# New durations in the planner that orders a two-layer encoder's small work between its large products

## The chip, the core and the metric

The kernel runs on one core of one Trainium2 chip. The metric is the device time of one execution in microseconds (us). It is the median of several runs. Five engines work side by side, each with its own instructions in program order: TensorE (PE) multiplies, VectorE (DVE), ScalarE (ACT) and GpSimd (POOL) do elementwise work, and SyncE (SP) issues the loads.

## What is computed

Two layers over 256 tokens of width 2048, in fp32. Each layer has a norm, one wide input projection, three mixers whose outputs are concatenated, an output projection, and a feed-forward block.

```python
def hybrid_layer(x, ...):
    h = rms_norm(x, norm_mix)
    z = jnp.einsum('bsd,de->bse', h, w_in)
    (ml_q, ml_k, ml_v, ml_o, ml_g, mla_cq, mla_ckv, dil_q, dil_k, dil_v) = jnp.split(...)
    y_a = mlstm_mixer(...)      # 4 heads
    y_b = mla_mixer(...)        # 6 heads
    y_c = dilated_mixer(...)    # 6 heads
    y = jnp.concatenate([y_a, y_b, y_c], axis=-1)
    x = x + jnp.einsum('bse,ed->bsd', y, w_out)
    h = rms_norm(x, norm_ff)
    u = jax.nn.relu(jnp.einsum('bsd,df->bsf', h, w_ff1))
    return x + jnp.einsum('bsf,fd->bsd', u * u, w_ff2)
```

## The kernel before

Every large product is made of three products of fp32r operands: each weight tile of 128x1024 is loaded (`wst`), ACT copies its high part (`whi`, L239), DVE subtracts to get the low part (`wlo`, L241), and PE multiplies high by high, high by low and low by high. `Weights.next()` (L248) splits three tiles ahead. PE's large products write the tile `g`: nine input groups a layer (`in_group`, L405; eight weight tiles each, 12 products of 512 columns a tile), then the output projection (`out_proj`, L1065) and four chunks of the feed-forward (`ffn`, L1089).

The mixers' small work runs between the products of the input groups. Each piece (`mla_head` L623, `dil_prep` L704, `dil_head` L732, `ml_head` L915 and others) is a Python generator, and each `yield` ends a step. The order of all instructions is fixed when the program is built, by the planner `Stream` (L117). It holds a clock `clk`, which each PE product moves on by its assumed cost (L193, L198), and for each of ACT, DVE and POOL the time at which it is thought to be free. `Engine.__getattr__` (L86) looks up an operation's cost as (fixed, per element) in `COST` (L76) and calls `issue` (L129): the operation starts at the latest of the engine's free time, the clock, and the ends of what the same task issued on other engines, each with `MARGIN` = 0.4 us (L70) added. So within one step an operation on DVE or POOL is thought to start after ACT's part of the step, whether it needs it or not. A task is due again at the latest of these ends (L157). `pump` (L165), called after every three products of a token group (L400), issues the next step of each task that is due.

```python
last = self.cur.last
t = max([self.free[name], self.clk] + [v for k, v in last.items() if k != name])
self.free[name] = t + cost
last[name] = t + cost + MARGIN
```

Where a result is needed at once, `until` (L173) issues the steps of all tasks in the order in which they are due, with no product between, and sets the clock to each due time. That happens at the six hooks at which an MLA head starts (`MLA_AT`, L69: after tiles 3 and 7 of groups 2, 3 and 4, so 48 products apart; L1011, L1028). A head takes 3 of the `HALF` = 7 buffers of the pool `half` from `mla_head`'s start to its end, so at most two heads are under way: the hook of head 2 waits until head 0 is over, and so on. The hooks are called first to sixth below. One MLA head's PE steps are, in order, `mla_z` (24 products), `nkT`, `qrT`, `mla_s`, `pT`, `oT`. Its step at L649 to L657 has six squares on ACT and four copies on DVE; its step at L668 to L674 has four copies on ACT (`nk`) and the three POOL operations of `apply_rope` (L528). PE's steps of a dilated pair start with `dqkT`, after `apply_rope` on POOL at L726. PSUM has four banks for the mixers' PE results; `give(m=1)` returns one in the plan as soon as its last reading is issued.

Of the kernel before, what the change touches and what calls it, by code (L numbers as in the profile page):

```python
# [11 lines left out]
F32R = mybir.dt.float32r  # L12
# [60 lines left out]
class Engine:  # L73


    COST = {  # L76
        "activation": (0.16, 0.00083), "copy": (0.07, 0.00083), "tensor_tensor": (0.07, 0.00104),
        "scalar_tensor_tensor": (0.13, 0.00104), "tensor_scalar": (0.07, 0.00080), "tensor_copy": (0.07, 0.00104),
        "tensor_reduce": (0.07, 0.00104), "tensor_tensor_reduce": (0.07, 0.00104), "reciprocal": (0.07, 0.0066),
        "tensor_tensor_scan": (0.07, 0.00104), "memset": (0.07, 0.0004),  # L80
    }

    def __init__(self, stream, name, engine):
        self.s, self.name, self.e = stream, name, engine

    def __getattr__(self, f):  # L86
        fn = getattr(self.e, f)
        if f not in self.COST:
            return fn

        def call(*args, **kw):
            out = kw["in_"] if f == "tensor_reduce" else kw["out"] if "out" in kw else args[0]
            n = math.prod(out.shape[1:])
            fixed, each = self.COST[f]
            if self.name == "pool":
                fixed, each = 0.15, 2 * each
            self.s.issue(self.name, fixed + each * n)
            return fn(*args, **kw)  # L98

        return call  # L100
# [16 lines left out]
class Stream:  # L117
# [8 lines left out]
        self.tasks = []  # L126
        self.room = room

    def issue(self, name, cost):  # L129
        last = self.cur.last  # L130
        t = max([self.free[name], self.clk] + [v for k, v in last.items() if k != name])
        self.free[name] = t + cost
        last[name] = t + cost + MARGIN

    def product(self, cost):
# [54 lines left out]

def mm(c, out, lhsT, rhs, start, stop):
    n = out.shape[-1]
    c.s.product(n / 2400.0 * (1 if lhsT.dtype == F32R else 4) + 0.0025)  # L193
    c.nc.tensor.matmul(out, lhsT, rhs, start=start, stop=stop)  # L194


# [128 lines left out]
def mm3(c, out, l, r, start, stop):  # L325

    mm(c, out, l[0], r[0], start, False)
    mm(c, out, l[0], r[1], False, False)
    mm(c, out, l[1], r[0], False, stop)
# [1006 lines left out]
```

## Time and profile before

| | us |
|---|---|
| median of 3 runs | 2157.25 |
| lowest, highest | 2154.41, 2159.11 |
| the profiled execution's time | 2155.49 |
| its span (first to last instruction) | 2153.3 |
| PE busy | 2119.8 |
| DVE busy | 1322.4 |
| ACT busy | 1082.3 |
| POOL busy | 110.4 |

The profile is of one execution. "Busy" of PE overlaps in the pipeline, so the pitch from one product's start to the next's is what counts. "Idle before" is the time an engine stood still ahead of an instruction, with what released it. The span's stages are: start to 36, the first layer's input groups and mixers to about 290, its output projection to 380, its feed-forward to about 1093; the second layer follows in the same way, with its input groups to about 1358 and the end at 2153.

### The profile page before, as it was taken

The page shows a single profiled execution, that of the slowest core. Times are in us where ns is not written, and L with a number is a line of the kernel's source. Part 1 is how long each engine was busy: PE and PEld are TensorE (multiplying, and loading weights), DVE is VectorE, ACT ScalarE, POOL GpSimd, SP SyncE. Part 2 cuts the span into 40 slices and gives each one's busy share as a digit, 9 for nine tenths or more (in the row PEclk, how much of TensorE's full clock was granted, in tenths as well). Part 3 has the DMA queues.
Part 4 walks back from the last instruction along what each step waited for, and adds up shares of the span by engine and source line. Part 5 has one row for each costly group of instructions (what it writes and reads, how often), then busy time and mean ns, then how long its engine had stood idle before and what let it go on. Part 6 is the DMA issues. An engine that isn't in the chain of part 4 may idle for free.

```text
span 2153.3 us, 28894 instructions
## 1 busy us (share of the span) xinstructions
PE 2119.8 (98%) x10848; PEld 1804.9 (84%) x10848; DVE 1322.4 (61%) x1963; ACT 1082.3 (50%) x1883; POOL 110.4 (5%) x142
## 2 busy tenths in 40 slices
PE   8999999999999999999999999999999999999999
PEld 6788888888888888888887888888888888888887
DVE  7668755655564565565557687556546655655654
ACT  5666655543453444454456676554434434534442
POOL 6112100000000000000001121000000000000000
PEclk9999999999999999999999999999999999999999
DMA  7544455566656666566554444556565666566565
GB/s 228 189 141 126 154 175 181 187 194 190 193 186 195 194 188 193 190 192 196 178 174 142 143 128 153 174 189 192 186 198 189 190 191 195 187 195 194 187 200 162
DMA packets 109004, 389.89 MB, mean 181 GB/s; under 512 B 12352, under 2 KB 12480, under 8 KB 108608
## 3 DMA queue, kind: packets, MB, share of 16 engines
q1 hardware_dynamic: 107136, 384.97, 56.6%
q10 hardware_dynamic: 1728, 3.07, 0.4%
q8 instruction: 85, 1.39, 0.3%
q14 instruction: 55, 0.45, 0.1%
HBM read 385.90 MB, written 2.10 MB: 180 GB/s over the span
## 4 chain that ended last, share of the span: by engine, by line
PE 89%; ACT 4%; DVE 3%; POOL 2%; issue 1%; DMA 1%; POOLq 0%; ACTq 0%; DVEq 0%; SPq 0%
PE g L194 84%; ACT junk L98 1%; PE mla_z L194 1%; ACT whi L98 1%; DVE wlo L98 1%; POOL acc L98 1%; PE oT L194 1%; POOL sq L98 1%; DMA wst<-w_in 1%; PE xT L200 0%; PE pT L200 0%; PE dil_s L194 0%; PE mla_s L194 0%; POOL rp L98 0%; ACT dil_z L98 0%
## 5 line engine op out<-in xcount | busy, mean ns | idle before, releaser
L98 DVE TENSOR_TENSOR wlo<-wst,whi 128x1024 fp32r<-128x1024 f32 (+2 forms) x732 | 889.5, 1224 | 317.4 <-ACT whi L98 307.7
L98 ACT CAST whi<-wst 128x1024 fp32r<-128x1024 f32 (+2 forms) x732 | 761.2, 1043 | 539.7 <-PE g L194 402.5
L194 PE MATMUL g<-whi,u 128*128 128x512 f32 x2048 | 633.4, 389 | 0.0
L194 PE MATMUL g<-xg,whi 128*128 128x512 f32 x2048 | 489.8, 391 | 0.0
L194 PEld LDWEIGHTS g<-whi,u 128*128 128x128 f32 x2048 | 384.5, 188 | 79.6
L194 PEld LDWEIGHTS g<-xg,whi 128*128 128x128 f32 x2048 | 376.4, 188 | 72.8
L194 PE MATMUL g<-wlo,u 128*128 128x512 f32 x1024 | 398.4, 389 | 0.0
L194 PE MATMUL g<-whi,xg 128*128 128x512 f32 (+1 forms) x1152 | 371.7, 389 | 6.3 <-ACT whi L98 6.3
L194 PEld LDWEIGHTS g<-xg,wlo 128*128 128x128 f32 x2048 | 263.1, 191 | 12.1 <-ACT xg L98 2.0
L194 PE MATMUL g<-xg,wlo 128*128 128x256 f32 x2048 | 267.4, 283 | 1.1 <-ACT xg L98 1.1
L194 PEld LDWEIGHTS g<-whi,xg 128*128 128x128 f32 x1152 | 215.5, 189 | 44.0 <-ACT whi L98 6.3
L194 PEld LDWEIGHTS g<-wlo,u 128*128 128x128 f32 x1024 | 192.3, 188 | 39.8
L194 PE MATMUL g<-wlo,xg 128*128 128x512 f32 (+1 forms) x576 | 222.0, 385 | 3.3 <-DVE wlo L98 3.3
L98 ACT COPY ev<-g 128x256 f32<-128x256 f32 x128 | 48.0, 375 | 340.7 <-PE g L194 340.7
L98 DVE TENSOR_TENSOR ev<-g,ev 128x256 f32<-128x256 f32 x128 | 54.4, 425 | 229.8 <-ACT ev L98 229.7
L194 PE MATMUL g<-whi,y 128*128 128x512 f32 x512 | 162.8, 393 | 0.0
L194 PEld LDWEIGHTS g<-wlo,xg 128*128 128x128 f32 x576 | 109.1, 189 | 23.3 <-DVE wlo L98 6.7
L194 PEld LDWEIGHTS g<-whi,y 128*128 128x128 f32 x512 | 96.1, 188 | 19.7
L194 PE MATMUL g<-wlo,y 128*128 128x512 f32 x256 | 99.7, 389 | 0.0
L98 DVE SCALAR_TENSOR_TENSOR x<-g,r,x 128x512 f32<-128x512 f32 x64 | 45.8, 751 | 83.2 <-PE g L194 83.2
L98 DVE SCALAR_TENSOR_TENSOR ev<-ev 128x256 f32<-128x256 f32 x128 | 54.4, 425 | 4.4
L194 PEld LDWEIGHTS g<-wlo,y 128*128 128x128 f32 x256 | 48.1, 188 | 9.5
(206 smaller groups left out, 1199.1 us busy)
## 6 DMA issues: line engine op xcount, KB each, us to landing
wst<-w_ff SPq DMA_DIRECT2D x512, 512.0 KB, 4.2
wst<-w_in SPq DMA_DIRECT2D x128, 512.0 KB, 3.7
wst<-w_out SPq DMA_DIRECT2D x64, 512.0 KB, 4.2
wst<-w_in SPq DMA_DIRECT2D x16, 336.0 KB, 3.0
wst<-w_mla SPq DMA_DIRECT2D x12, 416.0 KB, 3.1
xt<-xT SPq DMA_DIRECT2D x8, 256.0 KB, 5.1
x<-x SPq DMA_DIRECT2D x2, 1024.0 KB, 7.1
out<-x ACTq DMA_DIRECT2D x8, 256.0 KB, 2.2
```

Source lines behind the costliest of these rows:

```text
L98: return fn(*args, **kw)
L194: c.nc.tensor.matmul(out, lhsT, rhs, start=start, stop=stop)
```

## The change

The table `COST` and what uses it get other numbers. Costs on ACT and DVE gain about 0.03 to 0.17 us of fixed time (reciprocal, scan and squares differ more), and each operation's engine is thought free 0.08 us before its end (`OVERLAP`). An ACT operation that also sums (`accum_out`) costs 0.2 us more (`READ`). POOL's operations cost 0.3 us and four times the element rate, instead of 0.15 and twice. A product of fp32r costs n/2400 + 0.0133 us instead of n/2400 + 0.0025, and one of plain fp32 n/1200 + 0.0025 instead of n/600 + 0.0025. No instruction is added or removed; `MARGIN`, the hooks and the pools stay.

```diff
     COST = {
-        "activation": (0.16, 0.00083), "copy": (0.07, 0.00083), "tensor_tensor": (0.07, 0.00104),
-        "scalar_tensor_tensor": (0.13, 0.00104), "tensor_scalar": (0.07, 0.00080), "tensor_copy": (0.07, 0.00104),
-        "tensor_reduce": (0.07, 0.00104), "tensor_tensor_reduce": (0.07, 0.00104), "reciprocal": (0.07, 0.0066),
-        "tensor_tensor_scan": (0.07, 0.00104), "memset": (0.07, 0.0004),
+        "activation": (0.26, 0.00086), "copy": (0.19, 0.00084), "tensor_tensor": (0.155, 0.00105),
+        "scalar_tensor_tensor": (0.20, 0.00107), "tensor_scalar": (0.16, 0.00080), "tensor_copy": (0.155, 0.00104),
+        "tensor_reduce": (0.155, 0.00104), "tensor_tensor_reduce": (0.24, 0.00105), "reciprocal": (0.15, 0.0062),
+        "tensor_tensor_scan": (0.155, 0.00205), "memset": (0.07, 0.0004),
     }
+
+    OVERLAP, READ = 0.08, 0.2
...
             if self.name == "pool":
-                fixed, each = 0.15, 2 * each
-            self.s.issue(self.name, fixed + each * n)
+                fixed, each = 0.3, 4 * each
+            elif self.name == "act" and kw.get("accum_out") is not None:
+                fixed += self.READ
+            self.s.issue(self.name, fixed + each * n, self.OVERLAP)
...
-    def issue(self, name, cost):
+    def issue(self, name, cost, overlap):
         last = self.cur.last
         t = max([self.free[name], self.clk] + [v for k, v in last.items() if k != name])
-        self.free[name] = t + cost
+        self.free[name] = t + cost - overlap
         last[name] = t + cost + MARGIN
...
-    c.s.product(n / 2400.0 * (1 if lhsT.dtype == F32R else 4) + 0.0025)
+    c.s.product(n / 2400.0 + 0.0133 if lhsT.dtype == F32R else n / 1200.0 + 0.0025)
```

## Rows read from the trace of the kernel before

**Rows 1.** Page, part 1: busy us (share of the span), instructions of each engine

```profile
PE 2119.8 (98%) x10848; PEld 1804.9 (84%) x10848; DVE 1322.4 (61%) x1963; ACT 1082.3 (50%) x1883; POOL 110.4 (5%) x142
```

**Rows 2.** Windows: length, then busy PE, PEld, DVE, ACT, POOL, PE clock, DMA

```profile
36.50:290.00 253.50, 243.23 (x1328) 207.04 (x1328) 185.00 (x418) 167.61 (x460) 39.38 (x53) 0.99 0.48 153
...
1125.00:1358.00 233.00, 224.38 (x1213) 189.70 (x1212) 173.63 (x395) 154.08 (x425) 34.62 (x39) 0.99 0.45 142
1448.00:2149.00 701.00, 701.00 (x3562) 599.89 (x3561) 403.80 (x481) 308.45 (x381) 0.00 (x0) 1.00 0.60 190
```

**Rows 3.** PE's waits over the whole span: us in total, times, longest

```profile
PE pT L200 <- DVE sm_e L98: 5.4, 2, 2.9
PE dqkT L200 <- POOL dil_z L98: 4.4, 4, 1.2
PE g L194 <- DVE wlo L98: 3.3, 7, 0.8
PE ml_w L194 <- DVE qrT_sb L98: 2.0, 2, 1.0
```

**Rows 4.** PE timeline, third hook: start, us, operation, count, [idle before, releaser]

```profile
98.72 0.65 PE L200 MATMUL nkT<-const,nk 128*128 128x128 f32 x4 [0.25 <-ACT nk L98]
101.83 1.17 PE L200 MATMUL pT<-const,sm_e 128*128 128x128 f32 x4 [2.46 <-DVE sm_e L98]
...
103.67 0.58 PE L194 MATMUL oT<-p_hi,mla_vh 128*128 128x256 f32 x1 [0.25 <-ACT p_hi L98]
...
105.63 0.36 PE L194 MATMUL mla_z<-whi,lat_hl 128*128 128x192 f32 x1
```

**Rows 5.** Windows: the stretch after that wait, columns as in rows 2

```profile
101.20:108.00 6.80, 5.78 (x24) 4.92 (x25) 3.98 (x9) 3.06 (x6) 0.00 (x0) 0.50 0.08 29
```

**Rows 6.** PE timeline: the first of three large products, and what follows them

```profile
119.53 0.39 PE L194 MATMUL g<-whi,xg 128*128 128x512 f32 x1
...
120.21 0.60 PE L200 MATMUL pT<-const,sm_e 128*128 128x128 f32 x4
```

**Rows 7.** POOL timeline: the rope of the second dilated pair, first layer

```profile
238.22 3.25 POOL L98 TENSOR_TENSOR rp<-dil_z,drope 128x256 f32<-128x256 f32 x2 [28.24 <-DVE dil_z L98]
241.54 1.58 POOL L98 TENSOR_TENSOR dil_z<-rp,rp 128x256 f32<-128x256 f32 x1
```

**Rows 8.** PE timeline: that pair's first transposes

```profile
243.18 1.09 PE L200 MATMUL dqkT<-const,dil_z 128*128 128x128 f32 x8 [1.23 <-POOL dil_z L98]
```

**Rows 9.** Groups by line and form: busy us, mean ns, idle before

```profile
L98 POOL TENSOR_TENSOR rp<-dil_z,drope 128x256 f32<-128x256 f32 x12 | 17.9, 1511 | 108.2 <-DVE dil_z L98 102.2 <-DVE ml_den L98 6.0
L98 POOL TENSOR_TENSOR rp<-qr,rope 128x128 f32<-128x128 f32 x24 | 17.7, 758 | 191.7 <-DVE qr L98 155.1 <-DVE sm L98 36.6
...
L98 ACT ACTIVATE nk<-mla_z,rs_y 128x128 f32<-128x128 f32 x48 | 13.6, 370 | 1.1 <-DVE qr L98 1.0
```

**Rows 10.** ACT timeline: head 0's first square, and what follows its sixth

```profile
70.73 0.27 ACT L98 ACTIVATE junk<-mla_z 128x128 f32<-128x128 f32 x1
...
72.88 1.05 ACT L98 CAST whi<-wst 128x1024 fp32r<-128x1024 f32 x1
```

**Rows 11.** ACT timeline: head 2's last two copies before `nkT`

```profile
117.79 0.62 ACT L98 ACTIVATE nk<-mla_z,rs_y 128x128 f32<-128x128 f32 x2
```

**Rows 12.** PE timeline: head 2's `nkT`, and head 3's `pT` and `oT` at the sixth hook

```profile
122.91 0.60 PE L200 MATMUL nkT<-const,nk 128*128 128x128 f32 x4
...
155.21 0.60 PE L200 MATMUL pT<-const,sm_e 128*128 128x128 f32 x4
...
157.03 0.60 PE L200 MATMUL nkT<-const,nk 128*128 128x128 f32 x4
157.38 0.36 PE L194 MATMUL oT<-p_hi,mla_vh 128*128 128x256 f32 x1
158.18 0.25 PE L194 MATMUL mla_z<-whi,lat_hl 128*128 128x192 f32 x1
```

**Rows 13.** DVE timeline: head 3's softmax scaling, the input of that `pT`

```profile
153.60 0.84 DVE L98 TENSOR_SCALAR sm_e<-sm_e,sm 128x256 f32<-128x256 f32 x2
```

## Prediction

> **What bounds the kernel now.** I read the page's busy times first, then the windows by stage, then PE's list of waits, and last the timelines around the longest waits. PE is the bound: it is busy for 98% of the span, the next engine, DVE, for 61% [rows 1]. In the second feed-forward PE is busy in all of its 701 us [rows 2], so nothing that only reorders other engines can gain there. The two stretches of input groups and mixers are the only place with something to win: PE stands still for 253.50 - 243.23 = 10.3 us in the first layer and 233.00 - 224.38 = 8.6 us in the second [rows 2].
>
> The waits there have three kinds, and the change meets them differently [rows 3]. The first is a PE step that the plan put ahead of its data: `dqkT` after POOL, 4.4 us in four waits. The second is a hook that forces a head to its end, so that PE has no product to put between the head's steps: `pT` after `sm_e`, 5.4 us in two waits, both at the third hook. There the steps `nkT`, `pT`, `oT` and the new head's `mla_z` follow each other without a large product [rows 4]. Behind that wait TensorE ran at its lower level, 1.2 GHz, a granted clock of 0.50 through 6.80 us [rows 5]. At half clock PE's 5.78 busy us did what some 2.9 us would do at 2.4 GHz, so about 2.9 us a layer are lost to the clock as well. The third kind is a hand-over of a PSUM bank (`ml_w` after `qrT_sb`, 2.0 us in two) or a late weight tile (`wlo`, 3.3 us in seven). The planner's bookkeeping has no entry for the first of these: a bank is free in the plan when its reading is issued, before and after.
>
> **The change, part by part.** Product cost: three products of 512 columns take 120.21 - 119.53 = 0.68 us [rows 6], so 0.227 each. The plan counted 512/2400 + 0.0025 = 0.2158, and will count 0.2266. Its clock was 5% slow; a step due L us ahead stood 1.05 L later in real time, and will stand L later. Taken alone this makes each step earlier by 5%.
>
> The rope of a dilated pair: the plan gave three POOL operations on 256 elements 3 x (0.15 + 2 x 0.00104 x 256) = 3 x 0.682 = 2.05 us, and `dqkT` was due 0.4 later, at 2.45 us (2.57 us of real products). The trace has 238.22 to 243.12, that is 4.9 us [rows 7]. PE reached `dqkT` early and waited 1.23 us [rows 8]. The new plan gives 2 x (1.375 - 0.08) + 1.375 + 0.4 = 4.37 us, so `dqkT` moves back by 1.8 us, six or nine products since tasks are looked at every three. That is more than the longest wait of 1.2 us. Products of the same group fill it, and later ones of the dilated chain have a whole group and the first half of the output projection before them: y[12] and up are first read in its ninth weight tile, 8 x 12 x 0.227 = 21.8 us after the last group. So the 4.4 us should go; I keep 2.2 to 4.4 as bounds, since a weight split queued before the rope on DVE may shift it by one tile.
>
> An MLA head: for the step with six squares the plan gave 4 x 0.266 + 2 x 0.213 = 1.49 us on ACT, then margin, four DVE copies of 0.203, and margin: 3.10 us. The new table gives 2.91 + 0.4 + 0.91 + 0.4 = 4.62, 1.5 us more. The trace has 72.88 - 70.73 = 2.15 us for the squares with their read-outs [rows 10], between 1.49 and 2.91. For the step with `nk` and the rope, the plan starts POOL only after ACT's four copies and the margin: 1.06 + 0.4 + 3 x 0.416 + 0.4 = 3.1 us before, 1.24 + 0.4 + (2 x 0.758 + 0.838) + 0.4 = 4.4 after, 1.3 us more. The ten other waits of a head (two means, two rsqrt parts, split of q and k, split of qr, maximum, exponentials, scaling, split of p) gain 0.1 to 0.5 each, 1.7 together. The chain from `mla_z` to `oT` grows from 17.4 us in the plan (18.3 real) to 21.9: each head's PE steps stand up to 3.6 us later.
>
> They weren't early. Head 2's `nk` ended at 117.79 + 0.62 = 118.41 [rows 11] and its `nkT` ran at 122.91 [rows 12], 4.5 us later; head 3's `sm_e` was ready at 154.44 [rows 13] and its `pT` ran at 155.21. So here the longer durations repair no wait. They push the heads towards the hooks that force them.
>
> What that costs differs by hook. At the third, the head is already forced from its maximum on, and the wait is the chain's own length; I put 0.3 us more on it. At the fourth, the steps left after the third hook's forcing grow by only some 0.2 us net of the clock: 0. At the fifth, `pT` is already forced; 0.5 us. At the sixth, six large products lie between `pT` and `nkT`/`oT` [rows 12] and cover the split of p; pushed back by over 1.4 us, `pT` comes behind them, and PE waits their 6 x 0.227 = 1.4 us. Together 2.2 us a layer, 4.4 in all. No row shows a head pushed so; the bounds are 0 (the due times fall into the same three products, or are forced at the same place) and the price of the third hook's wait, 2.46 us [rows 4], at each of the fourth to sixth hooks in both layers, 6 x 2.46 = 14.8. I take the value by the products that stand between, since rows 12 show them.
>
> Bank hand-overs and weight splits: which task takes a freed bank, and which DVE step stands before a `wlo`, changes by chance. The loads on SP stay at the same products, but their staging buffers come free after `wlo`, and so behind whatever the plan puts before it. 0, with bounds from -2.0 (both `ml_w` waits gone) to +3.3 (the weight waits double) [rows 3].
>
> The feed-forward, the output projection, the dilated heads' scores with their bias and the smaller recurrent steps get new dues as well: nothing, since PE has products without gap there [rows 2] and each result is read 20 us or more later; if that cover went, a feed-forward tile would cost the added 0.4 us once a chunk, eight in all, 3.2 us.
>
> A rule that speaks against one price for POOL: `rp` on 256 elements took 1511 ns in the mean and on 128 elements 758 [rows 9], against 1.375 and 0.838 in the new table. The Trainium skill, page GPSIMD Engine Reference, section Specifications, says that POOL shares its SBUF interfaces with VectorE and contends with VectorE instructions that read two SBUF inputs. By it the rope's length depends on which subtraction runs beside it. The sum by it would keep some of the `dqkT` waits, at most 2.2 us; the sum above goes by the rows.
>
> **The sum.** 2155.5 (the profiled execution's own time; 2.2 us of it lie around the span of 2153.3) - 4.4 + 4.4 + 0 = 2155.5. The median of the runs before stands 1.8 us above that execution, which would make 2157.3. I take the middle, 2156.5.
>
> **The rivals.** Faster: the dues move within the same three products at the hooks, the heads are forced where they were, and only the premature steps are mended: -4.4 for `dqkT` and -2.0 for `ml_w`, 2149 to 2151. For it: POOL's old price is the only one that was off by more than half [rows 7]. It goes to about 2145 if the third hook's wait also gets shorter, so that the clock stays at 2.4 GHz behind it and the 2 x 2.9 us come back [rows 5]; against that, the heads only get later.
>
> Slower: the hooks. If heads 1, 2 and 3 reach hooks four to six with their exponentials still to do, PE waits there as at the third, 2.46 us each, 14.8 in all: 2155.5 - 4.4 + 14.8 = 2166. It decides where a head's `pT` isn't issued before the last six products in front of its hook. For it: 3.6 us of delay a head against 1.4 us of products in between [rows 12]. Against it: at each hook all due steps are issued and the clock jumps, which takes back what the younger head has lost. The Trainium skill, page TensorE: Matmul & The Clock Gate, section HAM oscillation, says that a gap in PE's work puts the array back to half clock, which has to be paid at each such gap. The trace agrees at the third hook [rows 4, 5]; by it each new long wait would add up to 2.9 us, 2172 if one more a layer did.
>
> No effect: the order hardly changes, since steps are placed in units of three products (0.68 us) and the differences per step are 0.1 to 0.5 us; then 2157. Against it, the rope and the squares, 1.3 to 1.9 us.
>
> **How the numbers follow.** A measurement of this kernel can tell 0.2%, 4.3 us, from no change. Forecast of gain and loss in balance 0.33 and no effect 0.08: 0.41 within 0.2%. Faster 0.31: the rival with `dqkT` mended and the hooks held. Slower 0.28: the hooks. The range goes from the clock's case, 2145, to somewhat above the hooks without a second loss of clock, 2168; the likeliest case's own range is 2151 to 2161.
>
> **What would show it.** `dqkT` after `dil_z` gone from PE's waits, or below 2 us, shows the rope's step right. Waits of `pT` grown above 5.4 us, or new ones of `mla_s`, show the hooks' price; fewer large products between `pT` and `oT` before the sixth hook's `mla_z` shows its place. A granted clock below 1.00 in more or fewer than two stretches shows the clock's part. PE busy for less than the whole of the last 701 us would prove the claim on the feed-forward wrong. A total under 2149 with the `pT` wait gone would mean that later estimates shorten a forced chain, which I hold unlikely.

## The result and the profile after

The changed kernel takes 2178.7 us (median of 4, 2177.1 to 2183.4) against 2156.5 us, a ratio of 1.0106 with a 95% interval of 1.0086 to 1.0125. It is slower by 22 us, outside the range that was given. Its profiled execution has a span of 2174.8 us, 21.5 more than before. Medians here leave out the few executions that took over 2300 us.

The windows of the changed kernel come first: the two stretches of input groups and mixers and the last feed-forward. Columns are as in [rows 2]: length, busy us of PE, PEld, DVE, ACT and POOL, granted clock, DMA. The first two reach somewhat further than those of [rows 2], so the second block has the kernel before over the same stretches.

```profile
36.63:310.00 273.37, 255.91 (x1375) 218.47 (x1375) 189.24 (x423) 173.44 (x467) 36.60 (x53) 0.97 0.46 147
1105.00:1385.00 280.00, 264.87 (x1412) 225.68 (x1411) 190.73 (x427) 175.65 (x468) 31.95 (x39) 0.97 0.44 140
1470.00:2171.00 701.00, 700.75 (x3561) 599.46 (x3559) 403.66 (x481) 308.19 (x380) 0.00 (x0) 1.00 0.60 190
```

```profile
36.50:300.00 263.50, 253.23 (x1377) 215.54 (x1377) 190.65 (x425) 172.83 (x467) 39.38 (x53) 0.99 0.49 155
1105.00:1364.00 259.00, 250.38 (x1368) 214.07 (x1367) 187.76 (x422) 170.85 (x465) 34.62 (x39) 0.99 0.46 145
```

The feed-forward is as full as before. In the other two PE stands still for 17.5 and 15.1 us, against 10.3 and 8.6, and the mean clock is 0.97, where it was 0.99. PE's waits, as in [rows 3]:

```profile
PE g L198 <- DVE wlo L102: 10.7, 9, 2.4
PE pT L204 <- DVE sm_e L102: 8.4, 2, 4.2
...
PE ml_At L204 <- DVE ml_A L102: 3.5, 2, 1.9
PE ml_aT L204 <- DVE ml_na L102: 3.3, 2, 2.5
PE mla_s L198 <- DVE ml_ql L102: 2.1, 2, 1.1
PE oT L198 <- DVE p_lo L102: 2.0, 6, 0.3
PE ml_w L198 <- DVE qrT_sb L102: 2.0, 2, 1.0
PE oT L198 <- ACT p_hi L102: 1.4, 6, 0.2
```

`dqkT` no longer waits for POOL (0.6 us for a DVE step are left). The `pT` waits grew from 5.4 to 8.4 us, the weight waits from 3.3 to 10.7, and `ml_At` is new. `oT` now waits at each of the fourth to sixth hooks, 0.6 us each; before, it did so at the fifth. Three forced runs of the first layer on PE's timeline (start, us, operation, count, idle before), the first hook, the third and the fourth:

```profile
68.65 0.38 PE L204 MATMUL ml_aT<-const,ml_na 128*64 128x128 f32 x2 [2.52 <-DVE ml_na L102]
68.87 0.38 PE L204 MATMUL krT<-const,kr 128*64 128x128 f32 x2
71.11 0.44 PE L204 MATMUL ml_At<-const,ml_A 64*128 64x64 f32 x2 [1.86 <-DVE ml_A L102]
71.48 0.53 PE L198 MATMUL mla_z<-whi,lat_hl 128*128 128x192 f32 x1
...
104.59 0.59 PE L198 MATMUL mla_s<-mla_k,mla_q 128*128 128x256 f32 x3 [1.07 <-DVE ml_ql L102]
...
110.21 1.09 PE L204 MATMUL pT<-const,sm_e 128*128 128x128 f32 x4 [4.20 <-DVE sm_e L102]
111.09 1.06 PE L204 MATMUL nkT<-const,nk 128*128 128x128 f32 x4
111.97 0.58 PE L198 MATMUL oT<-p_hi,mla_vh 128*128 128x256 f32 x1
...
128.74 0.39 PE L198 MATMUL g<-whi,xg 128*128 128x512 f32 x1
128.97 0.60 PE L204 MATMUL pT<-const,sm_e 128*128 128x128 f32 x4
129.40 0.60 PE L204 MATMUL nkT<-const,nk 128*128 128x128 f32 x4
130.24 0.39 PE L198 MATMUL oT<-p_hi,mla_vh 128*128 128x256 f32 x1 [0.24 <-ACT p_hi L102]
```

At the first hook the gates' transposes `ml_aT` and `ml_At` stand ahead of head 0's `mla_z`, and PE waits for both. Before, only `ml_aT` stood there; `ml_At` came behind the head's 24 products and three large ones, and PE didn't wait for it:

```profile
70.86 0.33 PE L200 MATMUL ml_At<-const,ml_A 64*128 64x64 f32 x2
```

At the third hook `mla_s` has come into the forced run, so no large product stands between it and `oT`. At the fourth, `pT` has come behind the last large product. Windows over the stretches that the clock's record shows at half:

```profile
69.40:76.20 6.80, 5.09 (x24) 5.00 (x25) 4.43 (x9) 4.30 (x11) 0.00 (x0) 0.50 0.25 79
106.90:113.70 6.80, 3.35 (x13) 2.84 (x14) 4.59 (x12) 3.22 (x10) 1.25 (x3) 0.50 0.24 73
250.30:253.70 3.40, 3.40 (x9) 2.65 (x8) 3.33 (x6) 1.61 (x2) 2.36 (x3) 0.50 0.58 157
```

Before, there was one such stretch a layer [rows 5]; now there are three in the first layer and two in the second, 34.1 us in all against 13.7. Each follows or holds a long wait of PE, but not every long wait has one: the same weight wait in the second layer, 2.36 us at 1329.29, is followed by none. The one at 250 follows a weight wait. Around it, from DVE's timeline, ACT's and PE's:

```profile
246.71 0.42 DVE L102 TENSOR_TENSOR y<-ml_yT,y 128x256 fp32r<-128x256 f32 x1 [1.41 <-ACT y L102]
247.20 0.69 DVE L102 TENSOR_TENSOR p_lo<-pT,p_hi 128x512 fp32r<-128x512 f32 x1
247.81 1.22 DVE L102 TENSOR_TENSOR wlo<-wst,whi 128x1024 fp32r<-128x1024 f32 x1
```

```profile
245.36 1.05 ACT L102 CAST whi<-wst 128x1024 fp32r<-128x1024 f32 x1
246.31 0.37 ACT L102 CAST y<-ml_yT 128x256 fp32r<-128x256 f32 x1
```

```profile
245.39 0.38 PE L204 MATMUL ml_yT<-const,ml_hs 128*128 128x128 f32 x2
245.60 0.60 PE L204 MATMUL pT<-const,sm_e 128*128 128x128 f32 x4
...
249.07 0.50 PE L198 MATMUL g<-wlo,xg 128*128 128x512 f32 x1 [2.42 <-DVE wlo L102]
```

The weight split `wlo` is queued on DVE behind `y` and `p_lo`, the low parts of PE's newest `ml_yT` and `pT`. These need ACT's copies first. PE was done with `ml_yT` at 245.77, but ACT took it up at 246.31, behind a weight copy `whi` of 1.05 us. So PE waits for a split that stood, in order, behind steps on PE's own last products, and these behind ACT's queue.

**Where the 21.5 us went.** I sort PE's waits of over 0.15 us, after its first products, by what released them: waits of `pT`, `oT`, `nkT`, `qrT`, `mla_s`, `krT`, `ml_aT` and `ml_At` for what they read ("heads and gates"), `g` for `wlo` ("weights"), other mixer steps for their data, and all waits of a mixer step for something it doesn't read ("hand-over" of a bank or of the queue). Low clock counts half its length.

| us | heads, gates | dqkT | weights | hand-over | half of low clock | sum |
|---|---|---|---|---|---|---|
| before | 9.1 | 4.4 | 2.6 | 3.6 | 6.8 | 26.5 |
| after | 18.7 | 0 | 9.9 | 5.6 | 17.0 | 51.2 |
| difference | +9.6 | -4.4 | +7.3 | +2.0 | +10.2 | +24.7 |

The sum overstates the span's 21.5 by 3 us. Waits that lie inside a low stretch, 10.3 us after and 1.9 before, are counted half too much, which is 4 us of it; what is left, 20.5, accounts for the loss. As an account it is good to some 5 us either way: in the twenty profiles of this case, the span less all of PE's waits from 37 us on, and less half of the low clock outside them, is 2125 to 2134 us.

### The profile page after: what moved, and what is told of

Same layout as the page of the kernel before. It is cut to its first block, busy times and chain, and to the rows that moved or that the text cites. A ratio compares the mean times of both kernels' runs of the same rounds, so it can differ in the third digit from the quotient of the medians.

```text
span 2174.8 us, 28896 instructions
## 1 busy us (share of the span) xinstructions
PE 2126.7 (98%) x10848; PEld 1810.9 (83%) x10848; DVE 1321.2 (61%) x1963; ACT 1085.9 (50%) x1883; POOL 106.4 (5%) x142
## 4 chain that ended last, share of the span: by engine, by line
PE 92%; ACT 2%; DVE 2%; POOL 1%; DMA 1%; issue 1%; SPq 0%; POOLq 0%; DVEq 0%; ACTq 0%
PE g L198 87%; PE mla_z L198 2%; PE oT L198 1%; ACT whi L102 1%; POOL acc L102 1%; DMA wst<-w_in 1%; POOL sq L102 1%; DVE wlo L102 1%; ACT junk L102 1%; PE mla_s L198 1%; PE pT L204 1%; PE ml_h L198 0%; PE xT L204 0%; DVE p_lo L102 0%; ACT p_hi L102 0%
## 5 line engine op out<-in xcount | busy, mean ns | idle before, releaser
L198 PEld LDWEIGHTS g<-xg,wlo 128*128 128x128 f32 x2048 | 263.1, 191 | 12.1 <-ACT xg L102 2.0
L198 PE MATMUL g<-wlo,xg 128*128 128x512 f32 (+1 forms) x576 | 222.8, 387 | 10.7 <-DVE wlo L102 10.7
```

## The experiments

All times are medians on the same terms; the ratio is against the kernel before on the same chip, with its 95% interval.

**Each part alone.** First POOL's price:

```diff
-                fixed, each = 0.15, 2 * each
+                fixed, each = 0.3, 4 * each
```

> The kernel before with POOL's new price alone (0.3 us and four times the element rate). Theory A, forced runs: the longer ropes push the MLA heads and the rope of k later, so that more of their steps fall into the runs that the hooks force, where PE has no product to fill with; that takes back the 4.4 us that the dqkT waits lose. Expect 2156 to 2163 us, dqkT waits below 1 us, and a wait of ml_At or ml_aT at the first hook of 2 us or more a layer. Rival B, convoys: the loss is weight splits queued behind mixer steps on DVE and ACT, which come from the ACT and DVE prices; then POOL's price alone only mends dqkT, 2151 to 2153 us, and wlo waits stay near 3.3 us.

2160.8 us, 1.0018 (1.0008 to 1.0028). As theory A has it: no wait of `dqkT` for POOL; instead `pT` waits 7.5 us, and `ml_At` at the first hook 3.9.

```profile
PE pT L200 <- DVE sm_e L98: 7.5, 2, 3.8
...
PE ml_At L200 <- DVE ml_A L98: 3.9, 2, 2.1
```

Next the prices of ACT and DVE (their fixed parts grow by 0.07 to 0.17 us) with the overlap and the read-out, of which the main lines are

```diff
-        "activation": (0.16, 0.00083), "copy": (0.07, 0.00083), "tensor_tensor": (0.07, 0.00104),
+        "activation": (0.26, 0.00086), "copy": (0.19, 0.00084), "tensor_tensor": (0.155, 0.00105),
...
-        self.free[name] = t + cost
+        self.free[name] = t + cost - overlap
```

and then the products' cost by itself:

```diff
-    c.s.product(n / 2400.0 * (1 if lhsT.dtype == F32R else 4) + 0.0025)
+    c.s.product(n / 2400.0 + 0.0133 if lhsT.dtype == F32R else n / 1200.0 + 0.0025)
```

> The kernel before with the new ACT and DVE prices, the overlap and the read-out alone; POOL's price and the products' cost as before. Theory A: a head's chain is planned 3.2 us longer, so it should carry the larger part of the loss: 2164 to 2172 us, pT and oT waits at the third to sixth hooks grown to 9 us or more together (7.1 us before), dqkT waits still about 4 us. Rival B: the loss sits here nearly whole, 2172 to 2182 us, with wlo waits of 8 us or more.

> The kernel before with the products' new cost alone. The planner's clock runs 5% faster against unchanged prices, so steps come earlier in products. Theory A: heads reach their hooks earlier, 2150 to 2156 us, with pT waits at the third hook below 5.4 us; dqkT waits grow, to 5 us or more. Rival B: no effect on the convoys, 2154 to 2160 us, and waits as before.

`table_alone` takes 2201.8 us, 1.0213 (1.0197 to 1.0228), worse than either theory said. Heads and gates wait 25.8 us, hand-overs 11.4, weights 8.6, and the clock is low for 51 us. `clock_alone` takes 2160.2 us, 1.0020 (1.0010 to 1.0029): not the gain of theory A. Its `pT` waits fall to 4.4 us as expected, but weight waits rise from 2.6 to 5.5, and `dqkT` waits 3.6 us for POOL, not the 5 or more that were expected. The three parts alone add up to 4 + 45 + 3 = 52 us, the whole change costs 22. They don't add.

**Each part undone**, in the changed kernel: the line of POOL's price, the line of the products' cost (each as it was before), and the read-out set to nothing.

> The changed kernel with POOL's old price: the new ACT and DVE prices with the new product cost. Told apart: what made table_alone 23 us slower than the whole change. If it is the product cost (later steps by 5% at the old clock), this comes near the whole change, 2168 to 2180 us, with dqkT waits of 3 us or more; if it is POOL's price, this stays near 2195 us or above.

> The changed kernel with the products' old cost, so with the slow clock: every due time stands 5% later in products. Theory A: slower than the change, 2184 to 2205 us, with heads and gates waiting over 20 us. If the products' cost doesn't matter: 2174 to 2182 us.

```diff
-    OVERLAP, READ = 0.08, 0.2
+    OVERLAP, READ = 0.08, 0.0
```

> The changed kernel without the 0.2 us for an ACT operation that also sums. Of the 2.3 us that ACT and DVE prices add to a head, the six squares and two exponentials lose 1.6. Theory A: a good part of the loss comes back, 2160 to 2172 us. Rival B: the read-outs are true durations (0.19 us in the trace), and without them DVE steps are queued too early; no gain, 2176 to 2184 us.

`pool_undone` takes 2197.6 us (1.0192, 1.0176 to 1.0208), `clock_undone` 2192.2 (1.0164, 1.0147 to 1.0181), `read_undone` 2167.7 (1.0052, 1.0037 to 1.0067). With the old cost of the products the loss is 13 us larger, as lateness predicts. The squares' and exponentials' read-outs are half of the loss, also as it predicts, though the trace has them at 0.19 us each. That POOL's longer price saves 19 us under the new table and costs 4 under the old one fits no theory of mine. It is the table and not the products' cost that turns the sign: with the new table and the old products' cost POOL's price still saves 10 (`table_alone` against `clock_undone`). The weight waits are 16.8 us without POOL's price and 9.9 with it, at other places, and behind two of them a layer (at 254.91 and 289.23 in the first) the clock falls.

**Later or earlier as such.** `MARGIN` shifts every step alike.

```diff
-MARGIN = 0.4
+MARGIN = 0.2
```

> The changed kernel with MARGIN 0.2 instead of 0.4 us, hooks as before. Each planned wait of a head gets 0.2 us shorter, over some 16 margins about 3 us a head, as much as the change added. Theory A: the heads reach the hooks about as early as before the change, 2150 to 2164 us, pT waits at the third hook near 5.4 us. Rival B: margins shorter than the data need add waits elsewhere, 2172 us or more.

2160.4 us, 1.0019 (1.0010 to 1.0029): 18 of the 22 us come back, with the new prices all in place; the clock is low for 23.9 us and weights wait 2.6. The `pT` waits stay at 7.3 us, unlike expected. The same knob on the old prices, to 0.6, 0.2, 0.44 and 0.36:

> The kernel before, old table and hooks, with MARGIN 0.6 instead of 0.4 us. The new prices' shape is absent; every step is only planned 0.2 us later, about 3 us over a head's 16 margins. Theory A, later steps cost time whatever makes them later: 2164 to 2182 us, waits of MLA heads and gates 14 us or more (9.1 us before, 18.7 after). Rival C, it is the new prices' own pattern that costs: 2152 to 2162 us.

> The kernel before with MARGIN 0.2. Every step is planned 0.2 us earlier. Theory A: fewer waits at the hooks (below 9.1 us for heads and gates), but dqkT after POOL waits more (4.4 us before, 5 to 6 here) since its step now comes earlier still: 2148 to 2157 us. If steps then come ahead of their data all over: above 2162 us.

> The kernel before with MARGIN 0.44 instead of 0.40 us: a fifth of the shift of before_margin60. Theory A, a smooth cost of lateness: a fifth of its loss of 23 us, about 5 us, 2157 to 2164 us. Rival D, coincidences: which step just passes a hook or a weight split decides, and a small shift costs as much as a large one, anywhere from 2150 to 2185, with waits at places other than those of before.

> The kernel before with MARGIN 0.36. Theory A, smooth: about 2154 us, on the way to what before_margin20 would have to be; since that one was 11 us slower than before, a smooth cost allows at most 2 us of loss here: 2153 to 2159 us. Rival D, coincidences: 2162 us or more, or 2149 or less.

| MARGIN, old prices | median us | ratio, 95% | heads, gates | hand-over | low clock |
|---|---|---|---|---|---|
| 0.20 | 2166.0 | 1.0042 (1.0025 to 1.0059) | 16.3 | 7.2 | 20.5 |
| 0.36 | 2156.1 | 0.9998 (0.9988 to 1.0007) | 9.0 | 5.9 | 10.2 |
| 0.40 | 2156.5 | 1 | 9.1 | 3.6 | 13.7 |
| 0.44 | 2163.9 | 1.0031 (1.0021 to 1.0042) | 10.2 | 8.2 | 17.1 |
| 0.60 | 2179.5 | 1.0108 (1.0093 to 1.0124) | 19.2 | 13.2 | 34.1 |

With 0.6 the old prices lose what the new prices lose with 0.4. Heads, gates and low clock carry as much of it; weights wait less and hand-overs more (13.2 us against 5.6):

```profile
PE pT L200 <- DVE sm_e L98: 6.4, 4, 2.9
...
PE ml_aT L200 <- DVE ml_na L98: 4.9, 2, 4.6
PE g L194 <- DVE wlo L98: 4.7, 9, 1.5
PE ml_At L200 <- DVE ml_A L98: 3.1, 2, 1.9
```

So steps planned 0.2 us later cost 23 us without the new prices' shape; rival C falls. But 0.2 us earlier costs 10, and its trace says where most of it lies: `ml_At`, now planned earlier, has come into the first hook's forced run ahead of `mla_z`. It waits 6.8 us in the two layers, and in the first the clock falls during the wait:

```profile
70.47 0.44 PE L200 MATMUL ml_At<-const,ml_A 64*128 64x64 f32 x2 [5.29 <-DVE ml_A L98]
```

The old plan lies at the flat bottom of a curve that rises both ways, and 0.04 us later already costs 7. Of rival D's ranges the one for 0.36 failed, and 0.44 came out where both theories had it. Lateness isn't the whole cause: which step stands in a forced run counts, and an earlier plan can bring one in too.

**The hooks.** The gates started after the first hook:

```diff
     kr = s.spawn(k_rope(c, z1))
-    s.spawn(ml_gates(c, z1))
...
         s.finish(kr)
         mla(0)()
+        s.spawn(ml_gates(c, z1))
```

> The changed kernel with the gates of the recurrent mixer started after the first hook instead of before it, hooks as before. At the first hook the forced run then holds the rope of k alone. Theory A: ml_aT and ml_At (6.8 us of waits in the two layers) and the low clock behind them (about 2.4 us a layer) leave, the later hooks keep theirs: 2164 to 2170 us. If the first hook is not a cause of its own, its waits turn up elsewhere: 2174 us or more.

2169.9 us, 1.0064 (1.0046 to 1.0082), 9 us better, at the edge of what was expected. The waits moved rather than left: `ml_aT` is gone, and `ml_At` waits 4.2 us at the second hook instead, where it stands ahead of head 1's `mla_z`:

```profile
84.16 0.44 PE L204 MATMUL ml_At<-const,ml_A 64*128 64x64 f32 x2 [2.07 <-DVE ml_A L102]
```

But the low clock falls from 34.1 to 13.7 us: two stretches of 6.8 us in the first layer, at 84.2 and 108.1, and none in the second. Then the hooks' places:

```diff
-MLA_AT = ((2, 3), (2, 7), (3, 3), (3, 7), (4, 3), (4, 7))
+MLA_AT = ((2, 4), (3, 1), (3, 6), (4, 3), (5, 0), (5, 5))
```

> The changed kernel with the six hooks five weight tiles apart instead of four and the first one a tile later. Theory A: a head has 60 products more or less to itself before a hook forces it (5 tiles of 12), so the waits of pT, oT, ml_aT, ml_At and mla_s at hooks, 18.7 us of the changed kernel's list, mostly go, and the low clock behind them: 2155 to 2164 us. Rival B: the wlo waits and the convoys stay whatever the hooks do: 2172 to 2180 us.

> The kernel before, old table, with the six hooks at the places of after_hooks5 (2147.9 us). Theory A, forced runs: the table costs time through the hooks; where the hooks leave room, old and new table should be within a few us of each other, and the old one keeps its dqkT waits of about 4 us: 2147 to 2154 us. Rival B, convoys: the old table is better placed everywhere, so it gains as much from the moved hooks as the new one did (31 us) or at least 15: 2126 to 2142 us.

`after_hooks5` takes 2147.9 us, 0.9962 (0.9949 to 0.9975): faster than both kernels. Its waits of heads and gates are 5.2 us, hand-overs 0.5, low clock 3.4:

```profile
PE g L198 <- DVE wlo L102: 12.5, 12, 2.3
...
PE ml_aT L204 <- DVE ml_na L102: 1.6, 1, 1.6
PE oT L198 <- DVE p_lo L102: 1.4, 4, 0.3
PE pT L204 <- DVE sm_e L102: 1.2, 2, 0.6
```

`before_hooks5` takes 2153.9 us, 0.9992 (0.9983 to 1.0002). With these hooks the new prices are the better ones by 6 us, and the intervals don't overlap. The old ones lose it in hand-overs, 12.3 us against 0.5. Three more places of the hooks under the new prices, `after_late_hooks`, `after_shift1` and `after_hooks6` in this order, and then `MARGIN = 0.3` with the places of `after_hooks5`:

```diff
-MLA_AT = ((2, 3), (2, 7), (3, 3), (3, 7), (4, 3), (4, 7))
+MLA_AT = ((2, 3), (2, 7), (3, 5), (4, 2), (4, 7), (5, 4))
+MLA_AT = ((2, 4), (3, 0), (3, 4), (4, 0), (4, 4), (5, 0))
+MLA_AT = ((2, 5), (3, 3), (4, 1), (4, 7), (5, 5), (6, 3))
```

> The changed kernel with its first two hooks where they were and the third to sixth moved five tiles apart from the second on. Theory A by place: the first hook keeps its waits (ml_aT and ml_At, 6.8 us in both layers) and the low clock behind them, some 5 us more; the third to sixth lose theirs. Expect 2156 to 2163 us, between 2147.9 and 2178.7, ml_aT and ml_At still above 4 us together. If the later hooks aren't the larger part: above 2168 us.

> The changed kernel with all six hooks one tile later and still four tiles apart. Theory A, by place: the gates have 12 products more before the first hook, so its waits go as in after_hooks5; a head's window is as short as before, so pT and oT keep their waits at the third to sixth hooks (11.8 us in the changed kernel). Expect 2162 to 2170 us. If only the first hook counts: 2148 to 2156 us.

> The changed kernel with the hooks six tiles apart, the first two tiles later than before. Theory A: with 120 products between a head's start and the hook that forces it there is nothing left to force; what remains are wlo and bank waits. The sixth head now starts a group later, still well ahead of its use in the output projection. Expect 2144 to 2152 us, against 2147.9 with five.

> The changed kernel with the hooks of after_hooks5 (2147.9 us) and MARGIN 0.3. Theory A says that a plan with shorter waits loses less: 2143 to 2149 us. What is left to win there is 5 us of heads and gates and 12 us of wlo. If the hooks' place is a matter of single coincidences, it may land anywhere up to 2165.

They take 2177.5 (1.0093, 1.0078 to 1.0108), 2191.4 (1.0164, 1.0148 to 1.0180), 2202.5 (1.0216, 1.0199 to 1.0232) and 2159.3 us (1.0011, 1.0001 to 1.0020). All four miss what the theory expected; the last lies where its rival of single coincidences had it. (A head is forced two hooks after its own, so 96 products later with four tiles between hooks, 120 with five and 144 with six; in `after_late_hooks` the third hook stands six tiles behind the second.) Room before the later hooks alone gains 1 us, with the first hook's 6.9 us of gates' waits still there and new ones in the recurrent heads. One tile later alone takes most of the first hook's waits away (0.9 us of `ml_aT` is left) and gives `pT` 12.1 us. Six tiles push work behind the last input group, where the output projection forces it; PE's timeline and the window there:

```profile
309.69 0.74 PE L204 MATMUL ml_yT<-const,ml_hs 128*128 128x128 f32 x2 [2.50 <-DVE ml_hs L102]
310.89 0.80 PE L198 MATMUL g<-whi,y 128*128 128x512 f32 x1 [0.46 <-ACT y L102]
```

```profile
299.50:316.50 17.00, 12.56 (x35) 9.71 (x36) 6.41 (x17) 4.87 (x11) 0.00 (x0) 0.50 0.10 31
```

So where the hooks stand decides tens of us, but more room is no rule; five tiles was a good place, not an instance of one.

## Why the prediction was wrong

**Right.** The bound and the place: all but some 0.3 us of the loss lies in the input groups and mixers, none in the feed-forward. The rope of a dilated pair: `dqkT` after `dil_z` is gone from the list, 4.4 us, the upper of the two bounds. (Its reading of the room behind is off without harm: y[12] is first read in the output projection's eleventh weight tile, not its ninth.) POOL's own times did vary, from 0.77 to 1.73 us for a rope step of 256 elements in the kernel before, but one longer price was enough. The heads get later and the hooks charge for it: the forecast +4.4 us has +9.6 in its place, with the gates' share.

**The steps that failed.** First, the list of hooks. It priced the third to the sixth and left out the first, where no head is forced but the rope of k is, and with it whatever is due earlier, here the gates. Of the +9.6 us, `ml_aT` and `ml_At` are 3.3 + 3.5 - 1.8 = 5.0, where `ml_aT`'s one wait before was 1.8 us. `pool_alone` shows POOL's price alone bringing `ml_At` in. At the third hook I put 0.3 us a layer; in the first layer `pT` went from 2.46 [rows 4] to 4.20, and `mla_s` got a wait of 1.07 (a hand-over), since `mla_s` itself moved into the forced run. The sixth hook's 1.4 us came out as 0.6 of `oT` waits, and the fourth's 0 as 0.6 too; the fifth had 0.6 before and kept it, without the 0.5 more. The next head's `nkT` stands in between and covers part of the split.

Second, the clock. The forecast had no change of it, and the slower rival one more loss of 2.9 us a layer. It measured +10.2 us, the largest item as counted, 6 of it outside the waits. Its low stretches follow long waits, and they come behind a weight wait and the first hook too, not at the third hook alone [rows 5].

Third, the weight splits: 0, with a bound of +3.3. They measured +7.3. I took the in-order queue of DVE as chance that evens out. Of the 7.3 us, 4.8 are the new wait at 249 and its like in the second layer, where `ml_yT` and `pT` ran 0.2 us apart and `wlo` was queued behind their splits; the rest lies at earlier weight tiles. That later due times make such meetings likelier is my reading, and no run shows it by itself.

**The rivals.** The slower one named the mechanism at the hooks and the clock, 2166 to 2172 us, and 2178.7 lies above it. The point it said decides, `pT` behind the last products before a hook, held at the fourth to sixth hooks, but at the price of 0.6 and not 2.46 us. That its 14.8 us for them come near the 16.9 that heads, gates and weights gained together is luck: the first hook and the weights weren't in it. It had 0.28, the forecast 0.33; the range ended at 2168.

**What stays open.** Why POOL's longer price costs 4 us under the old prices and saves 19 under the new, a difference as large as the whole loss. The overlap was never run apart from the other prices of ACT and DVE. The sums of waits say where each plan loses, but not by which rule the coincidences fall, and no run here took a single coincidence out by itself except the first hook's, whose wait moved to the second. So where the loss lies is shown; why the steps meet there is in part argued.

## What to carry to other kernels

A planner that places steps by estimated durations isn't improved by truer estimates alone: hooks and margins that suited the old ones have to be fitted again with the new (here five tiles and the new prices, 8 us better than the kernel before). One such fit is a trial, not a rule: with four tiles from the same first hook, or six, the kernel was 35 and 46 us slower than the kernel before. Before such a change, list every place at which the plan is forced, the first included, and ask of each what else is due by then. And look at how ready the data already is: steps that run us after their input have nothing to gain from later estimates.

## What was not expected of the hardware

Beside 34.2 us of waits the changed kernel loses 17.0 to the clock, half the length of its low stretches. In `table_alone` the granted clock was at half, 1.2 GHz, for 51 us in all, one stretch of it 13.60 us long:

```profile
108.90:122.50 13.60, 9.59 (x43) 9.02 (x44) 7.52 (x18) 6.73 (x20) 1.78 (x3) 0.50 0.13 41
```

PE was at work for 9.59 us of that stretch and stood still for the rest, 2.92 us of it for `pT`. The same program also varies in this: executions of `after_late_hooks` had a mean clock of 0.996 at 2172.5 us and 0.992 at 2177.2 to 2177.9. Its waits above are read from the faster one.
